# Shift and scale multiplied from unsplit weights in four column groups, and the modulation sums one product later

## The chip, the cores and the metric

One Trainium2 chip, one of its cores. The time is the device time of one execution in microseconds (us); the median of several runs counts. Traces are one profiled execution each, taken by the hardware profiler.

## The reference

Two transformer blocks over 256 tokens of 1024 features, in float32, with 256 context tokens beside them in the first block. Only its opening matters here:

```python
m_l = (silu(c) @ w_ada + b_ada)[:, None, :]       # of the tokens; w_ada is 1024 x 6144
m_c = silu(c_ctx) @ w_ada + b_ada                 # of the context
sh1, sc1, g1, sh2, sc2, g2 = jnp.split(m_l, 6, axis=-1)
csh1, csc1, *_ = jnp.split(m_c, 6, axis=-1)
hl = rmsnorm(lat, norm_g0) * (1.0 + sc1) + sh1
hc = rmsnorm(cx, norm_g0) * (1.0 + csc1) + csh1
... = jnp.split(h @ w_in, 5, axis=-1)             # q, f forward, f backward, v, g
```

Then come the HGRN2 mixer (a gated scan in both directions), the sum `lat + g1 * y`, a convolutional feed-forward part, and a second block of retention, windowed attention and an MLP. Only the token rows go on after the mixer.

## The kernel before

Everything runs on one core, and TensorE is kept supplied by a single stream of weights. The order of the work is written out by hand: instructions stand on each engine in the order in which the Python code emits them.

**The stream.** All weights are listed once, in the order of use, as chunks of one or two halves of up to 128 x 1024 numbers. `pump` (L115) walks that list: SP's queue issues the load of a half into one of eight `raw` buffers, as soon as the half eight places earlier is done with; then ScalarE (ACT) copies it to `hi` in float32r (L154), and VectorE (DVE) writes `lo = raw - hi` (L155), so that `hi + lo` is exact. A product is three float32r multiplications, hi times hi, hi times lo and lo times hi (`mm3`, L355 to L357, in these rows with the activations `hTh` and `hTl`). A half of kind "split" gives its raw buffer back when it is split, one of kind "raw" when its readers are done. `use` (L166) takes the next chunk and runs `pump`.

**The opening.** `xT` holds context and tokens with features on partitions, 512 columns for each of eight tiles k of 128 features. DVE and ACT square and add them (L452 to L456), four small multiplications (L466) sum over partitions, DVE and POOL make the reciprocal root `r` (POOL's power at L322), DVE puts `r` on four diagonals `dg` (L471), and a multiplication by ones (L480) spreads it over all partitions in PSUM; `x_r` multiplies a tile by it (L405). For each k, `ada_mm(k)` (L396) multiplies `silu` of the two conditioning vectors by the 1024 x 256 weights that give shift and scale of the 128 features of tile k. The vectors stand in `c4` as four columns, hi and lo of each, so that 16 multiplications of 4 output rows by 256 columns, hi (L399) and lo (L400) of the weights, make a result of four rows; ACT copies it to `rs` (L402). `feat(k)` (L407) multiplies `rs` by the small matrix `sel`, which adds the rows of one vector and turns the result so that features lie on partitions (L409, L410); DVE makes the factors `AB` (L412, L413); ACT and DVE write the normed tile in two parts, `hTh` and `hTl`.

**The steps.** The first product of the mixer, the gates of two heads (four output tiles `e` of 512 columns), is summed over k as the tiles get ready. Step k multiplies tile k by chunk `f0_k`; `plan` (L493) sets what else is emitted in it: "0s123a" is output 0, then `s` (feat and splits of tile k + 1), outputs 1 to 3, then `a` (`ada_mm(k + 2)`). In the stream the two halves of `ada` k + 2 stand between `f0_k` and `f0_k+1`.

**The rest of the modulation.** The other columns of `w_ada` are multiplied on DVE, a row tile at a time, into `vr`, between the mixer's products (`ada_step`, L559). When a part is complete, a function that finishes it waits in `pending` until `ada_flush` (L579). For g1 that is `ada_rows` (L588): two multiplications by ones that sum `vr` over partitions (L592, 512 columns each), each followed by an addition on DVE (L593).

**The gate product.** The last of the mixer's four head pairs has its small products among the columns of the gate product `g`, which has four parts p: `slots` (L862) puts the transposes T, the scores SC, the states S and the outputs O into it, one slot after every four k tiles. `SC_` (L631) multiplies 32-column stationary parts, with 128 rows, into the four 32-partition quarters of a bank (L640, L642); `S_` (L622) reads `kcT`, which ACT copies from the transposes (L620). After part p = 1 the code calls `ada_flush` (L878). PSUM banks with the tag `x` are four, taken in turn by these small products, by `ada_rows` and by `ada_mm`.

```python
        z = fm_product(C["g", p], x=lambda k: hT(k, 256, 512), tag="m", ticks=1)
        drain()
        if p == 1:
            ada_flush()
```

Of the kernel before, what the change touches and what calls it, by code (L numbers as in the profile page):

```python
# [13 lines left out]
OP = mybir.AluOpType  # L14
# [17 lines left out]
LAG2 = 3  # L32

# [17 lines left out]
def kernel(ctx: ExitStack, tc: tile.TileContext, a, out):  # L51
# [17 lines left out]
    # A chunk is one or two halves of up to 1024 columns. A half is loaded, then split exactly into two  # L69
    # float32r parts, hi + lo.  # L70
    halves, chunks = [], []

    def add(hs, kind="split"):
        """hs: per half (parts, k tiles, columns); a part is (view of the half's tile, source)."""
        first = len(halves)
        for parts, k, n in hs:
            halves.append((parts, k, n, kind))
            assert k * n <= 1024, (k, n)
        chunks.append((first, len(halves)))
        return len(chunks) - 1  # L80
# [4 lines left out]
    def kpc(src):  # L85
        return src.rearrange("(k p) c -> p k c", p=128)
# [13 lines left out]
    class SplitPool:  # L100
        """Buffers for the two parts of bufs halves, for the halves under limit."""
# [13 lines left out]
    def pump(limit, hold=False):  # L115
        """Issue the loads and the splits that have a free buffer, splits of halves under limit only."""
# [49 lines left out]
    def use(i, keep=None, ahead=None):  # L166
        """The k tiles of chunk i as a list of (hi, lo); chunks before it (or before keep) are done with."""
# [17 lines left out]
    def part_done(i):  # L185
        """The first half of chunk i is done with."""
        at_["rel"] = max(at_["rel"], chunks[i][0] + 1)
        pump(len(halves))

# [24 lines left out]
    def ada_chunk(k):  # L214
        C["ada", k] = add([([(lambda t, s=s: t[:, :, s * 128:(s + 1) * 128],
                              kpc(w_ada[j * 512:(j + 1) * 512, s * D + k * 128:s * D + (k + 1) * 128]))
                             for s in range(2)], 4, 256) for j in range(2)])
# [5 lines left out]
    for k in range(KT):  # L223
        C["f0", k] = add([([(lambda t, d=d: t[:, 0, d * 256:(d + 1) * 256],
                             w_in[k * 128:(k + 1) * 128, (1 + d) * D:(1 + d) * D + 256])
                            for d in range(2)], 1, 512)])
        if k + 2 < KT:
            ada_chunk(k + 2)
# [72 lines left out]
    sel = early.tile([4, 2], F32, name="sel")  # L301
# [22 lines left out]
    def rstd_of(ms, width=1, n=1):  # L324
        """(ms / n + eps) ^ -0.5; ms [128, width], or [128, 2] to be added."""
# [8 lines left out]
    def mean_sq(junk, x, ms):  # L334
        """ms = the part of the mean over D of x ^ 2 that x holds."""
        s_.activation(junk, x, AF.Square, scale=D ** -0.5, accum_out=ms)
# [43 lines left out]
    def fm_product(chunk, nk=KT, x=None, tag="x", ticks=0):  # L380
        """Two feature tiles of a product over lat tokens -> one bank [128, 2, T]."""
# [14 lines left out]
    def ada_mm(k, w):  # L396
        rw = bank("x")
        for kk in range(KT):
            t_.matmul(rw[:4, :256], c4[:, kk, :], w[kk][0], start=kk == 0, stop=False)  # L399
            t_.matmul(rw[:4, :256], c4[:, kk, :], w[kk][1], start=False, stop=kk == KT - 1)  # L400
        rs[k] = p0.tile([4, 256], F32, tag="rs", name="rs")
        return lambda: s_.activation(rs[k], rw[:4, :256], AF.Copy)  # L402
# [44 lines left out]
    # rstd of the tokens, then the same on every partition  # L447
    sq = [p0.tile([128, 512], F32, tag="sq", name="sq", bufs=8) for _ in range(KT)]
    c4 = early.tile([128, KT, 4], F32R, name="c4")
    for k in range(KT):  # L450
        if k < 2:
            v_.tensor_mul(sq[k], xT[:, k, :], xT[:, k, :])  # L452
        else:
            s_.activation(sq[k], xT[:, k, :], AF.Square)
            v_.tensor_add(sq[k % 2], sq[k % 2], sq[k])
    v_.tensor_add(sq[0], sq[0], sq[1])  # L456
    v_.tensor_mul(cs, cs, vecs[:, 0:16])
    for j in range(2):
        v_.tensor_copy(c4[:, :, 2 * j], cs[:, 8 * j:8 * j + 8])
        v_.tensor_tensor(c4[:, :, 2 * j + 1], cs[:, 8 * j:8 * j + 8], c4[:, :, 2 * j].bitcast(F32),  # L460
                         op=OP.subtract)
# [8 lines left out]
    for i in range(4):  # L470
        v_.tensor_scalar(dg[:, i, :], ident, r[:, i:i + 1], None, op0=OP.mult)  # L471
# [20 lines left out]
    # products of the gates, with the sums (a), the features (s) and the next weights' splits among them  # L492
# [66 lines left out]
    def ada_step(parts=(3, 4, 2)):  # L559
        """One chunk of the rest of the modulation: sums over k on each partition, then over partitions."""  # L560
# [146 lines left out]
    for p in range(4):  # L707
# [59 lines left out]
        def gates(d):  # L767
            kt_ = kk_[d]
            # ctx: k times the decay from its token to the end of the scan
# [15 lines left out]
            # lat: sums of log f within chunks of 64  # L785
# [38 lines left out]
            # tokens of a block in order: forward [A, B], backward [B, A], A scanned first;  # L824
            # the middle slot holds q of B from the block's start, k of A to the block's end
# [33 lines left out]
    # the last pair's products among those of the gate, as its factors get ready  # L859
# [13 lines left out]
    for p in range(4):  # L873
# [4 lines left out]
        if p == 1:  # L878
            ada_flush()
# [14 lines left out]
    def row_product(name, n, lhs, done):  # L894
        """Sums over k tiles of two; lhs(j, kk, tok) gives the stationary parts. The last chunks
        are taken token tile by token tile, so that the first tile's rows are finished early; done(tok, acc)
        is stepped as the halves of a tile's rows get ready, its last step gives what has to follow."""
# [64 lines left out]
    def to_hT(pool, n, tok, A, B=None, tag="hf"):  # L962
        """n [128, D] token rows -> hT columns of the token tile, times A (plus B) per feature.
        A bank is read by one engine only."""
# [29 lines left out]
    def scaled(dst, src, r):  # L994
        """dst = src * r, a half on each of two engines."""
# [29 lines left out]
    def split_rows(cs_, mid, first):  # L1025
        """The products of chunks of columns token tile by token tile, the second after mid(), which comes
        behind the first chunks of the first; gives what turns them, features on partitions."""
# [49 lines left out]
    def ffn_done(tok, acc):  # L1077
# [11 lines left out]
        # with v = mean(x^2) + eps, x v^-.5 g is the block's result, and its own norm u (mean(u^2) + eps v)^-.5  # L1089
# [18 lines left out]
    def conv(z, m, name):  # L1108
        """z [128, 2, T]: centred taps over the tokens of tiles m, m + 1."""
# [53 lines left out]
    # ---------------- second block: projections  # L1163
# [151 lines left out]
    # softmax and retention among the projections, a step after each four k tiles  # L1315
# [126 lines left out]
def _pack(inputs):  # L1442
    """The small vectors with features on partitions: column j of a vector holds features 128 j .. 128 j + 127."""
# [13 lines left out]
def _shape_constants():  # L1457
    ident = np.eye(128, dtype=np.float32)
    sel = np.array([[1, 0], [1, 0], [0, 1], [0, 1]], np.float32)
# [36 lines left out]
```

## Time and profile before

| | |
|---|---|
| time, median of 3 runs | 888.44 us (887.88 to 889.48) |
| profiled execution, span from first to last instruction | 886.7 us, 15396 instructions |
| profiled execution's own time | not listed apart from its span; the median lies 1.7 us above that |
| PE (matmul) busy | 863.0 us, 97% |
| PEld (weight load) busy | 781.0 us, 88% |
| DVE, ACT, POOL busy | 618.6, 512.9 and 17.3 us |
| bytes moved | 161.98 MB, 183 GB/s over the span |

Engines: PE is TensorE, PEld its weight loads, DVE is VectorE, ACT is ScalarE, POOL is GpSimd, SP the queue that issues most loads. Matmuls are pipelined, so that a row's duration includes the way through the array; the distance between starts is what one costs in a run of them. A multiplication of float32 operands is one instruction in the program and two records in the trace.

### The profile page before, as it was taken

The page shows a single profiled execution, that of the slowest core. Times are in us where ns is not written, and L with a number is a line of the kernel's source. Part 1 is how long each engine was busy: PE and PEld are TensorE (multiplying, and loading weights), DVE is VectorE, ACT ScalarE, POOL GpSimd, SP SyncE. Part 2 cuts the span into 40 slices and gives each one's busy share as a digit, 9 for nine tenths or more (in the row PEclk, how much of TensorE's full clock was granted, in tenths as well). Part 3 has the DMA queues.
Part 4 walks back from the last instruction along what each step waited for, and adds up shares of the span by engine and source line. Part 5 has one row for each costly group of instructions (what it writes and reads, how often), then busy time and mean ns, then how long its engine had stood idle before and what let it go on. Part 6 is the DMA issues. An engine that isn't in the chain of part 4 may idle for free.

```text
span 886.7 us, 15396 instructions
## 1 busy us (share of the span) xinstructions
PE 863.0 (97%) x6144; PEld 781.0 (88%) x6144; DVE 618.6 (70%) x955; ACT 512.9 (58%) x823; POOL 17.3 (2%) x27
## 2 busy tenths in 40 slices
PE   4999999999999999999999999999999999999997
PEld 2679897988978999999998799999999899999995
DVE  7876878776888778977767736766486587555532
ACT  6877575673857575655545745756463575444431
POOL 1000000000000000000000000000000000000000
PEclk9999999999999999999999999999999999999999
DMA  9984472733634458776764374445596087656401
GB/s 313 276 280 167 131 250 78 258 116 116 216 122 156 154 192 294 253 246 208 236 213 95 122 225 138 130 141 158 184 312 195 24 285 243 191 190 190 161 1 47
DMA packets 131967, 161.98 MB, mean 183 GB/s; under 512 B 14136, under 2 KB 114488, under 8 KB 131896
## 3 DMA queue, kind: packets, MB, share of 16 engines
q1 hardware_dynamic: 129728, 155.80, 55.0%
q10 hardware_dynamic: 2168, 5.20, 1.7%
q8 instruction: 48, 0.79, 0.3%
q14 instruction: 23, 0.19, 0.1%
HBM read 159.93 MB, written 1.05 MB: 182 GB/s over the span
## 4 chain that ended last, share of the span: by engine, by line
PE 91%; ACT 3%; DVE 3%; DMA 2%; issue 1%; POOL 0%; SPq 0%; POOLq 0%; DVEq 0%; ACTq 0%
PE m L355 17%; PE m L356 17%; PE m L357 17%; PE x L355 8%; PE x L357 8%; PE x L356 8%; PE x L684 2%; DMA xT<-in_xcT_dram 1%; PE m L345 1%; PE x L345 1%; PE m L346 1%; PE m L341 1%; PE x L626 1%; PE x L346 1%; DMA raw<-in_hg_w_in_dram 1%; PE x L341 1%
## 5 line engine op out<-in xcount | busy, mean ns | idle before, releaser
L155 DVE TENSOR_TENSOR lo<-raw,hi 128x1024 fp32r<-128x1024 f32 (+1 forms) x264 | 310.0, 1204 | 134.0 <-ACT hi L154 131.0
L154 ACT ACTIVATE hi<-raw 128x1024 fp32r<-128x1024 f32 (+1 forms) x264 | 265.7, 1038 | 121.1 <-PE x L356 51.0
L355 PE MATMUL m<-hTh,hi 128*128 128x256 f32 (+1 forms) x560 | 178.8, 319 | 0.6 <-ACT hTh L425 0.6
L356 PE MATMUL m<-hTl,hi 128*128 128x256 f32 (+1 forms) x560 | 171.7, 307 | 0.2 <-DVE hTl L432 0.2
L357 PE MATMUL m<-hTh,lo 128*128 128x256 f32 (+1 forms) x560 | 171.4, 306 | 0.0
L355 PE MATMUL x<-hTh,hi 128*128 128x256 f32 x592 | 166.2, 281 | 0.0
L356 PE MATMUL x<-hTl,hi 128*128 128x256 f32 x592 | 165.1, 279 | 0.0
L357 PE MATMUL x<-hTh,lo 128*128 128x256 f32 x592 | 165.1, 279 | 0.0
L355 PEld LDWEIGHTS m<-hTh,hi 128*128 128x128 f32 x560 | 105.8, 189 | 9.2 <-issue 2.9
L355 PEld LDWEIGHTS x<-hTh,hi 128*128 128x128 f32 x592 | 111.2, 188 | 1.0 <-ACT hi L154 0.2
L356 PEld LDWEIGHTS x<-hTl,hi 128*128 128x128 f32 x592 | 110.8, 187 | 1.0 <-issue 0.2
L357 PEld LDWEIGHTS x<-hTh,lo 128*128 128x128 f32 x592 | 111.2, 188 | 0.0
L356 PEld LDWEIGHTS m<-hTl,hi 128*128 128x128 f32 x560 | 105.8, 189 | 5.7 <-DVE hTl L432 0.8
L357 PEld LDWEIGHTS m<-hTh,lo 128*128 128x128 f32 x560 | 105.4, 188 | 5.8 <-DVE lo L155 0.4
L355 PE MATMUL m<-hi,ah 128*128 128x512 f32 x248 | 97.2, 392 | 0.0
L357 PE MATMUL m<-hi,al 128*128 128x512 f32 x248 | 96.8, 391 | 0.0
L356 PE MATMUL m<-lo,ah 128*128 128x512 f32 x248 | 96.5, 389 | 0.0
L357 PEld LDWEIGHTS m<-hi,al 128*128 128x128 f32 x248 | 46.5, 188 | 10.6 <-DVE al L1141 0.4
L356 PEld LDWEIGHTS m<-lo,ah 128*128 128x128 f32 x248 | 46.6, 188 | 8.9
L355 PEld LDWEIGHTS m<-hi,ah 128*128 128x128 f32 x248 | 46.6, 188 | 8.9 <-ACT ah L1137 0.2
L355 PE MATMUL m<-hi,hTh 128*128 128x256 f32 x128 | 36.2, 283 | 0.0
L575 DVE SCALAR_TENSOR_TENSOR vr<-raw,cs,vr 128x1024 f32<-128x1024 f32 x28 | 35.8, 1280 | 0.4
(302 smaller groups left out, 1267.4 us busy)
## 6 DMA issues: line engine op xcount, KB each, us to landing
raw<-in_ffn_w_up_dram SPq DMA_DIRECT2D x44, 512.0 KB, 5.7
raw<-in_w_in_dram SPq DMA_DIRECT2D x42, 512.0 KB, 3.6
raw<-in_hg_w_in_dram SPq DMA_DIRECT2D x36, 512.0 KB, 4.9
raw<-in_w_ada_dram SPq DMA_DIRECT2D x32, 512.0 KB, 4.9
raw<-in_w_up_dram SPq DMA_DIRECT2D x32, 512.0 KB, 4.7
raw<-in_w_down_dram SPq DMA_DIRECT2D x32, 512.0 KB, 3.6
raw<-in_ffn_w_down_dram SPq DMA_DIRECT2D x22, 512.0 KB, 4.5
raw<-in_w_ada_dram SPq DMA_DIRECT2D x32, 256.0 KB, 4.5
```

The lines of the kernel that those rows point to most:

```text
L154: s_.activation(h[:, :w], r[:, :w], AF.Copy)
L155: held.append(lambda r=r, h=h, l=l, w=w: v_.tensor_tensor(l[:, :w], r[:, :w], h[:, :w].bitcast(F32), op=OP.subtract))
L341: t_.matmul(o, hTl[:, k, c], w[k][0], start=False, stop=k == KT - 1)
L345: t_.matmul(o, hTh[:, k, c], w[k][0], start=k == 0, stop=False)
L346: t_.matmul(o, hTh[:, k, c], w[k][1], start=False, stop=False)
L355: t_.matmul(o, wh, xh, start=start, stop=False)
L356: t_.matmul(o, wh, xl, start=False, stop=False)
L357: t_.matmul(o, wl, xh, start=False, stop=stop)
L575: v_.scalar_tensor_tensor(acc, w[kk][0], cs[:, k:k + 1], acc, op0=OP.mult, op1=OP.add)
L626: t_.matmul(z[:, d * 128:(d + 1) * 128], kcT[hh][:, (2 * d + j) * 128:(2 * d + j + 1) * 128], vt[:, j, hh * 128:(hh + 1) * 128], start=j = ...
L684: t_.matmul(z[:, b * 128:(b + 1) * 128], l, r, start=i == 0, stop=i == len(terms) - 1)
```

## The change

- `w_ada`'s columns for the first shift and scale are laid out on the host (`ada1`), so that a half is one load with 4 KB per partition, and so are the `f0` chunks (`f0w`, 2 KB per partition); before, a half of either was two loads.
- The `ada` chunks are of kind "raw": they are not split, and the multiplication is of plain float32.
- `c4` (four float32r columns) gives way to `c2`, 32 float32 columns of which two are filled. `ada_mm` multiplies k tile kk into the partitions 32 (kk mod 4) to 32 (kk mod 4) + 31 of a bank, and `sel`, now 128 x 2, adds the four groups. `rs` has 128 rows.
- 36 multiplications of `ones` by `ones` (float32, 128 columns) stand ahead of the first sums, into a bank that nothing reads.
- `silu` of the vectors is computed after the fourth square, not after the last; the diagonals `dg` take one DVE instruction, not four.
- `ada_flush` is called after part p = 2 of the gate product, not after p = 1.

```diff
+WARM = 36
     def ada_chunk(k):
-        C["ada", k] = add([([(lambda t, s=s: t[:, :, s * 128:(s + 1) * 128],
-                              kpc(w_ada[j * 512:(j + 1) * 512, s * D + k * 128:s * D + (k + 1) * 128]))
-                             for s in range(2)], 4, 256) for j in range(2)])
+        C["ada", k] = add([([(whole, a["ada1"][k, :, j])], 4, 256) for j in range(2)], "raw")
...
-        C["f0", k] = add([([(lambda t, d=d: t[:, 0, d * 256:(d + 1) * 256],
-                             w_in[k * 128:(k + 1) * 128, (1 + d) * D:(1 + d) * D + 256])
-                            for d in range(2)], 1, 512)])
+        C["f0", k] = add([([(whole, a["f0w"][k])], 1, 512)])
...
-    sel = early.tile([4, 2], F32, name="sel")
+    sel = early.tile([128, 2], F32, name="sel")
...
         for kk in range(KT):
-            t_.matmul(rw[:4, :256], c4[:, kk, :], w[kk][0], start=kk == 0, stop=False)
-            t_.matmul(rw[:4, :256], c4[:, kk, :], w[kk][1], start=False, stop=kk == KT - 1)
-        rs[k] = p0.tile([4, 256], F32, tag="rs", name="rs")
-        return lambda: s_.activation(rs[k], rw[:4, :256], AF.Copy)
+            g = slice(kk % 4 * 32, kk % 4 * 32 + 32)
+            t_.matmul(rw[g, :256], c2[:, kk, :], w[kk][0], start=kk < 4, stop=kk >= 4)
+        rs[k] = p0.tile([128, 256], F32, tag="rs", name="rs")
+        return lambda: s_.activation(rs[k], rw[:, :256], AF.Copy)
...
-    c4 = early.tile([128, KT, 4], F32R, name="c4")
+    c2 = early.tile([128, KT, 32], F32, name="c2")
+    v_.memset(c2, 0.0)
+    wb = bank("x")
+    for _ in range(WARM):
+        t_.matmul(wb[:, 0:128], ones, ones, start=True, stop=True)
...
+        if k == 3:
+            for j in range(2):
+                v_.tensor_mul(c2[:, :, j], cs[:, 8 * j:8 * j + 8], vecs[:, 8 * j:8 * j + 8])
+            v_.tensor_mul(cs, cs, vecs[:, 0:16])
     v_.tensor_add(sq[0], sq[0], sq[1])
-    v_.tensor_mul(cs, cs, vecs[:, 0:16])
-    for j in range(2):
-        v_.tensor_copy(c4[:, :, 2 * j], cs[:, 8 * j:8 * j + 8])
-        v_.tensor_tensor(c4[:, :, 2 * j + 1], cs[:, 8 * j:8 * j + 8], c4[:, :, 2 * j].bitcast(F32),
-                         op=OP.subtract)
...
-    for i in range(4):
-        v_.tensor_scalar(dg[:, i, :], ident, r[:, i:i + 1], None, op0=OP.mult)
+    v_.tensor_tensor(dg, ident.rearrange("p (o c) -> p o c", o=1).to_broadcast([128, 4, 128]),
+                     r.rearrange("p (i o) -> p i o", o=1).to_broadcast([128, 4, 128]), op=OP.mult)
...
-        if p == 1:
+        if p == 2:
             ada_flush()
...
-    sel = np.array([[1, 0], [1, 0], [0, 1], [0, 1]], np.float32)
+    sel = np.tile(np.eye(32, 2, dtype=np.float32), (4, 1))
...
+    ada = np.asarray(inputs["w_ada"])[0, :, :2 * D].reshape(2, 4, 128, 2, KT, 128)
+    data["ada1"] = ada.transpose(4, 2, 0, 1, 3, 5).reshape(KT, 128, 2, 4, 256)
+    f0w = np.asarray(inputs["hg_w_in"])[0, :, D:3 * D].reshape(KT, 128, 2, D)[..., :256]
+    data["f0w"] = f0w.reshape(KT, 128, 1, 512)
```

What stands on PE between two outputs of a step: first the end of step 0 before (of the 16 multiplications of `ada_mm` eight are shown; the lines of the changed kernel are three fewer there than before), with `c_150` the columns `c4`,

```order
L356 MATMUL m<-hTl,hi 128x512
L357 MATMUL m<-hTh,lo 128x512
L399 MATMUL x<-hi,c_150 4x256
L400 MATMUL x<-lo,c_150 4x256
L399 MATMUL x<-hi,c_150 4x256
L400 MATMUL x<-lo,c_150 4x256
L399 MATMUL x<-hi,c_150 4x256
L400 MATMUL x<-lo,c_150 4x256
L399 MATMUL x<-hi,c_150 4x256
L400 MATMUL x<-lo,c_150 4x256
```

and the same place in the changed kernel, with `c_142` the 32 columns of `c2`, as far as the feat of the next step:

```order
L353 MATMUL m<-hTl,hi 128x512
L354 MATMUL m<-hTh,lo 128x512
L397 MATMUL x<-raw,c_142 32x256 x8
L352 MATMUL m<-hTh,hi 128x512
L353 MATMUL m<-hTl,hi 128x512
L354 MATMUL m<-hTh,lo 128x512
L406 MATMUL x<-sel,rs 128x2
L407 MATMUL x<-sel,rs 128x2
```

Eight multiplications read the raw weights where 16 read their two parts; nothing else on PE moved within a step.

ACT in two steps of the opening, before (`h` and `hTh` are the features, `rs` the result of `ada_mm`, `hi` the weights' upper parts):

```order
L154 ACTIVATE hi<-raw 128x1024
L402 ACTIVATE rs<-x 4x256
L154 ACTIVATE hi<-raw 128x512
L154 ACTIVATE hi<-raw 128x1024
L423 ACTIVATE h<-xT,AB 128x256 x2
L428 ACTIVATE hTh<-h 128x512
```

and in the changed kernel:

```order
L399 ACTIVATE rs<-x 128x256
L155 ACTIVATE hi<-raw 128x512
L420 ACTIVATE h<-xT,AB 128x256 x2
L425 ACTIVATE hTh<-h 128x512
```

The two copies of 1024 columns per step are gone, and with them, on DVE, the two subtractions; the split of `f0` still stands ahead of the features.

PE at the end of part p = 1 of the gate product, before (the scores SC of the last head pair, then `ada_rows`, then part p = 2):

```order
L642 MATMUL x<-qe,ke 32x32
L645 MATMUL x<-Q,K 128x128
L651 MATMUL x<-Q,K 64x64 x2
L592 MATMUL x<-vr,ones 128x512 x2
L355 MATMUL m<-hTh,hi 128x256
L356 MATMUL m<-hTl,hi 128x256
```

and in the changed kernel, at the end of part p = 2:

```order
L643 MATMUL x<-qe,ke 32x32
L646 MATMUL x<-Q,K 128x128
L652 MATMUL x<-Q,K 64x64 x2
L593 MATMUL x<-vr,ones 128x512 x2
L352 MATMUL m<-hTh,hi 128x256
L353 MATMUL m<-hTl,hi 128x256
```

The two sums, and on DVE their two additions, stand 48 multiplications and four small products later; at the end of p = 1 the scores are followed by part p = 2 at once.

## Rows read from the trace of the kernel before

**Rows 1.** The page's chain that ended last, by engine.

```profile
PE 91%; ACT 3%; DVE 3%; DMA 2%; issue 1%; POOL 0%; SPq 0%; POOLq 0%; DVEq 0%; ACTq 0%
```

**Rows 2.** Waits of PE, whole span: total us, times, longest us.

```profile
PE x L592 <- ACT kcT L620: 1.8, 1, 1.8
...
PE x L409 <- ACT rs L402: 0.6, 1, 0.6
```

**Rows 3.** Timeline, step 4: start us, duration us, engine, line, out<-in.

```profile
45.05 0.39 PE L355 MATMUL m<-hTh,hi 128*128 128x512 f32 x1
...
45.84 0.38 PE L409 MATMUL x<-sel,rs 4*128 4x2 f32 x2
...
46.37 0.50 PE L355 MATMUL m<-hTh,hi 128*128 128x512 f32 x1
...
48.57 0.28 PE L399 MATMUL x<-hi,c 128*4 128x256 f32 x1
...
48.78 0.69 DVE L432 TENSOR_TENSOR hTl<-h,hTh 128x512 fp32r<-128x512 f32 x1
...
50.39 0.39 PE L355 MATMUL m<-hTh,hi 128*128 128x512 f32 x1
```

**Rows 4.** Timeline of all engines, from the first sums to the last step.

```profile
13.48 0.37 PE L399 MATMUL x<-hi,c 128*4 128x256 f32 x1
...
13.91 2.05 POOL L322 TENSOR_TENSOR r<-r,mhalf 128x4 f32<-128x4 f32 x1 [13.46 <-DVE r L330]
...
16.66 0.41 PE L400 MATMUL x<-lo,c 128*4 128x256 f32 x1
...
16.92 2.02 PE L480 MATMUL x<-dg,ones 128*128 128x512 f32 x2
16.93 2.95 DVE L155 TENSOR_TENSOR lo<-raw,hi 128x1024 fp32r<-128x1024 f32 x3
...
19.80 0.68 DVE L405 TENSOR_TENSOR xT<-xT,x 128x512 f32<-128x512 f32 x1
...
21.97 0.50 PE L355 MATMUL m<-hTh,hi 128*128 128x512 f32 x1 [0.56 <-ACT hTh L425]
...
61.88 0.39 PE L357 MATMUL m<-hTh,lo 128*128 128x512 f32 x1
```

**Rows 5.** Timeline of PE, scores in four 32-column groups of the array.

```profile
96.47 0.40 PE L357 MATMUL m<-hTh,lo 128*128 128x512 f32 x1
96.80 0.24 PE L640 MATMUL x<-qe,ke 128*32 128x64 f32 x1
...
96.82 0.25 PE L642 MATMUL x<-qe,ke 128*32 128x32 f32 x3
...
97.16 0.49 PE L645 MATMUL x<-Q,K 128*128 128x128 f32 x2
```

**Rows 6.** Timeline of PE, one float32 product of 256 columns: both records, then the first alone.

```profile
531.41 0.59 PE L1220 MATMUL x<-ks,qs 64*128 64x256 f32 x2
...
531.41 0.38 PE L1220 MATMUL x<-ks,qs 64*128 64x256 f32 x1
```

**Rows 7.** Windows: stretch, length, busy us by engine, granted clock, DMA share, GB/s.

```profile
13.40:16.80 3.40, 3.40 (x18) 1.85 (x17) 2.45 (x8) 2.48 (x3) 2.05 (x1) 1.00 1.12 344
...
250.90:254.20 3.30, 3.30 (x11) 2.27 (x11) 3.30 (x5) 1.10 (x2) 0.00 (x0) 0.50 0.30 102
```

**Rows 8.** Timeline around the modulation sums: PE, ACT, DVE.

```profile
247.72 1.12 PE L592 MATMUL x<-vr,ones 128*128 128x512 f32 x2
250.62 1.88 PE L592 MATMUL x<-vr,ones 128*128 128x512 f32 x2 [1.78 <-ACT kcT L620]
...
264.56 0.39 PE L355 MATMUL m<-hTh,hi 128*128 128x256 f32 x1
...
249.98 1.08 ACT L620 ACTIVATE kcT<-x 128x512 f32<-128x512 f32 x2
...
250.88 1.22 DVE L155 TENSOR_TENSOR lo<-raw,hi 128x1024 fp32r<-128x1024 f32 x1
```

## The prediction

> **What bounds the kernel now.** I read the chain that ended last first, then PE's waits, then the stretches that the change touches. PE carries 91% of the chain that ends last [rows 1], in a span of 886.7 us. PE's waits are few: the longest in the body of the kernel is 1.8 us, of the modulation sums on ACT's `kcT`; the next one in the opening is 0.6 us, of a feat on `rs` [rows 2]. So microseconds taken off PE come off the time, as long as ACT, DVE and the loads keep up, and I look at three places: the start, the eight steps of the opening, and the sums for g1.
>
> In a step of the opening the reader is to see that PE is full: from 45.05 to 50.39, 5.34 us, three products, the feat at 45.84, nine products from 46.37 to 48.57 (0.24 us each), sixteen small ones of `ada_mm` from 48.57 to 50.39 (1.82 us, 0.114 each), and the next step follows at once [rows 3]. The steps run from 21.97 to 61.88 and 0.23 for the last product: 40.1 us [rows 4]. Without waits they would take six times 5.34, once 3.52 (step 6, no `ada_mm`) and once 2.9 (step 7, no feat): 38.4 us. So 1.7 us are waits, mostly in the first three steps, where splits on ACT and DVE hold things up.
>
> **The steps.** `ada_mm` becomes eight float32 products of 256 columns, 16 records. Two such records took 0.59 and one 0.38, so they follow each other by 0.21 us [rows 6]. What is not plain is whether four column groups run at once. The scores show it: 16 records, of which a group with 64 columns has four, began at 96.80, the first of each group by 96.82, and the next full-width product began at 97.16 [rows 5]. One after the other, at 0.21 per 256 columns, eight records of 64 and eight of 32 columns would take 0.64 us; four at once, 0.21, which leaves 0.15 for start and end. The scores also began 0.33 after a product that costs 0.24, 0.09 late. So `ada_mm` should take 0.09 + 4 x 0.21 + 0.15 = 1.1 us instead of 1.82. For the six in the steps: 6 x 0.72 = 4.3 us saved.
>
> The Trainium skill ("TensorEngine Tiling (Array Packing)", Key Properties) says that a change of the tiling mode drains the array; the 0.09 and the 0.15 are what this trace shows of it. Its page "TensorE: Matmul & The Clock Gate" (Measured speedup vs the span model) gives a speedup of 3.07 for four row tiles, not 4; an estimate from that page is 1.3 us instead of 1.1, and 1.4 us less saved over the six.
>
> Of the 1.7 us of waits I take 1.5 as gone. ACT loses two copies per step and DVE two subtractions; only the features' own chain stays, and it fits: feat to next step's second product is now 0.53 + 9 x 0.24 + 1.1 + 0.24 = 4.0 us, against 3.6 us from the feat at 45.84 to the end of `hTl` at 49.47 [rows 3]. What is late next would be that chain, with 0.4 us of slack. **Together 5.8 us;** bounds 3.0 (a group costs half again as much and the waits stay) and 6.0.
>
> **The loads.** A step needs 1.31 MB. With the queue full, 344 GB/s were moved even in the present short pieces [rows 7], 3.8 us per step against a new pace of 4.6, and the pieces get longer. A raw half is now held until PE has multiplied it, not until DVE has split it, and SP issues in order, so the third `f0` load waits for `ada_mm(1)`. Eight buffers are two and two thirds steps, some 12 us, which covers the load. I take nothing; the queue behind SP is a rival below.
>
> **The start.** Sixteen products from 13.48 to 16.66 are 0.21 us apart [rows 4], where the same ones take 0.114 later [rows 3]: half pace, 1.2 GHz against 2.4, although the window prints 1.00 [rows 7]; where the page prints 0.50, the pace is the same. The added 36 products are 72 records of 128 columns, 0.105 us each at full clock and 0.21 at half. They can begin near 1.1. If the clock rises after as long as the 0.50 stretch lasted, 3.3 us [rows 7], 16 records go at half and 56 at full: done at 10.3, before the squares at about 12. If it takes twice as long, done at 11.8. All at half would be 16.2.
>
> Then the sums run at full pace, which with three small products moved into DVE's chain of squares brings POOL's power (13.91) forward by some 0.3 us; and `x_r` no longer waits for three subtractions (16.93 and 2.95) but follows the spread `r`, which ends at 18.94: 0.8 earlier than 19.80 [rows 4]. That makes 1.1. If the spread too ran at full pace it would be 1.0 more. But `ada_mm(0)` is shorter now, so PE idles for POOL's 2.05 us between it and the spread; an idle time of 1.78 was followed by a granted clock of 0.50 [rows 7, 8]. So I expect half pace again, and charge 0.4 for the first products of step 0 (1.4 if all of them are slow). **0.7 us;** bounds -0.3 and 2.1.
>
> **The modulation sums.** Before, the first of the two sums ran at 247.72; the second needed a bank that ACT had not yet emptied, and began at 250.62 after 1.78 us of idle. Then 3.3 us went by at a granted clock of 0.50, half of it lost, and part p = 3 began at 264.56 [rows 7, 8]. Of the 16.84 us between, 1.78 + 1.65 are loss and 13.4 are work. All this work remains, in another order. What is late next: part p = 2 starts at 247.8, twelve products take 1.4 us, and then the states S need the same `kcT`, whose first half ACT ends at about 250.5, and soon after the `lo` that DVE ends at 252.1 [rows 8]. ACT and DVE do not wait for PE there, so this does not move: 1.3 + 0.5 = 1.8 us of new idle. At the new place, after p = 2, the banks that the sums take were emptied long before, and DVE's two additions fall where it has idle time. **Saved: 16.84 - 13.4 - 1.8 = 1.6 us,** if the clock stays. PE idled 0.6 us once without a loss of clock [rows 2] and 1.78 once with it; 1.3 is between. I take it as staying, since it is shorter than the only one that cost the clock; if not, nothing is saved. Bounds 0 and 3.4.
>
> **Sum.** 5.8 + 0.7 + 1.6 = 8.1 us, so a span of about 878.6. The median before, 888.44, lies 1.7 above the profiled span, and I take the same here: **880.3 us**. By the bounds: 11.5 saved, 876.9, and 2.7 saved, 885.7.
>
> **Rivals.**
>
> 1. *The two records of a product hold back the next group.* The trace speaks against it: four groups' first records began within 0.02 us, before any second one could [rows 5]. If it were so here, with 256 columns, a group would start when the one before is half done: 9 x 0.21 + 0.24 = 2.1 us per `ada_mm`. The steps would lose 6 x 0.3 = 1.8, gain the 1.5 of waits, the start would lose 0.5 of its 0.7: 1.4 saved in all, 887.0, no change that can be told. The Trainium skill's page "TensorE: Matmul & The Clock Gate" (The mechanism) has matmuls start and end strictly in program order; by that rule this rival would hold, and these rows differ from it. Chance 0.06.
> 2. *Wide streams do not run side by side at all.* The rows in four groups are of 32 and 64 columns; four streams of 256 float32 columns at once are not in this trace. In a row they cost 16 x 0.21 + 0.24 = 3.6 us, 1.78 more than now; six make 10.7, `ada_mm(1)` 1.5 more ahead of step 0; against 1.5 + 0.7 + 1.6 saved that is 8.4 lost: 896.8. It decides from 1.82 us per `ada_mm` on. Chance 0.06.
> 3. *SP's order starves the steps.* If each step waits for its load and keeps 5.34 us, only the start and the sums save, 2.3: 886.1. Against it stand 344 GB/s and the eight buffers. Chance 0.05.
> 4. *The added products outlast the squares* and end at 16.2: 3.9 of the 8.1 are lost, 884.2. Chance 0.03.
>
> **How the numbers follow.** My forecast has 0.80. The range, 876.5 to 885.5, takes in its bounds, less a few tenths at the worst end where all three would have to fail together, and rival 4; it leaves out the first three. A measurement of this kernel can tell some 0.2%, 1.8 us, from no change: its three runs spread over 1.6. Faster by more than that is below 886.7: the forecast, rivals 3 and 4, 0.88. Within it: rival 1, 0.06. Slower: rival 2, 0.06.
>
> **What would show it.** Each `ada_mm` as 16 records that begin in groups of four and take 1.0 to 1.2 us up to the next full-width product, steps of 4.6 us, the first at about 20.9, the last ending near 55.5. No subtraction of 1024 columns on DVE in the opening. A short wait of PE on `kcT`, by the states S, and no wait of the modulation sums. A granted clock of 1.00 after it. It would be wrong if `ada_mm` takes 2 us or more, if PE waits for DMA or for `hi` in the steps, or if steps and start save their share and the stretch from 56 to 240 gives it back.

## The result and the profile after

The changed kernel takes 880.29 us (median of 4 runs, 877.26 to 882.56); the kernel before takes 888.16 us beside it (median of 4, 887.13 to 889.48). The ratio is 0.9906, interval 0.9886 to 0.9927. The prediction was 880.3 us. The total was met, but not term by term: the start was put too low, the steps and the sums too high, and by luck these misses nearly cancel.

The profiled run is the fastest of the four: 877.26 us with a span of 875.5 us. Its chain still lies on TensorE, with a smaller share than [rows 1]. From the page:

```profile
PE 89%; DVE 5%; ACT 3%; DMA 1%; issue 1%; POOL 0%; SPq 0%; POOLq 0%; DVEq 0%; ACTq 0%
```

PE's waits, to be read against [rows 2] (total us, times, longest us):

```profile
PE m L352 <- ACT hTh L422: 1.5, 1, 1.5
PE x L627 <- ACT kcT L621: 1.4, 1, 1.4
...
PE x L481 <- DVE dg L471: 1.1, 1, 1.1
...
PE x L699 <- DVE on L693: 0.5, 1, 0.5
...
PE x L685 <- ACT xs L665: 0.4, 1, 0.4
```

The sums' own wait of 1.8 us is gone from the list. The states S (L627) wait for `kcT` instead, as the prediction had it. Two waits later in the same stage are new: O (L685) and its transposes (L699). In the start PE now waits for `dg` and for the first features.

The start, to be read against [rows 4]. Timelines of PE, DVE, POOL and ACT (start us, duration us, engine, line):

```profile
12.02 1.03 PE L467 MATMUL x<-ones,sq 128*128 128x2 f32 x8
12.98 1.07 PE L397 MATMUL x<-raw,c 128*32 128x256 f32 x16
15.13 1.12 PE L481 MATMUL x<-dg,ones 128*128 128x512 f32 x2 [1.08 <-DVE dg L471]
...
19.12 0.50 PE L352 MATMUL m<-hTh,hi 128*128 128x512 f32 x1 [1.52 <-ACT hTh L422]
...
25.62 0.50 PE L352 MATMUL m<-hTh,hi 128*128 128x512 f32 x1
```

```profile
13.34 1.02 POOL L319 TENSOR_TENSOR r<-r,mhalf 128x4 f32<-128x4 f32 x1 [12.90 <-DVE r L327]
...
15.68 0.63 ACT L155 ACTIVATE hi<-raw 128x512 fp32r<-128x512 f32 x1 [1.17 <-DMA raw<-in_f0w_dram]
...
16.34 0.69 DVE L156 TENSOR_TENSOR lo<-raw,hi 128x512 fp32r<-128x512 f32 x1 [1.10 <-ACT hi L155]
...
16.95 0.68 DVE L402 TENSOR_TENSOR xT<-xT,x 128x512 f32<-128x512 f32 x1
```

The sums, the small products and the spread run at full pace: 1.03, 1.07 and 1.12 us, where the spread took 2.02 [rows 4]. The first gate product stands at 19.12 us instead of 21.97, and step 1 begins at 25.62. What held `x_r` (L402) was no longer three subtractions but one, L156, behind a load.

Step 4 and the last gate product, to be read against [rows 3] and [rows 4] (timeline of PE and DVE):

```profile
38.87 0.50 PE L352 MATMUL m<-hTh,hi 128*128 128x512 f32 x1
...
39.44 0.40 PE L354 MATMUL m<-hTh,lo 128*128 128x512 f32 x1
39.67 0.28 PE L406 MATMUL x<-sel,rs 128*128 128x2 f32 x2
39.81 0.36 PE L407 MATMUL x<-sel,rs 128*128 128x2 f32 x2
40.03 0.47 PE L352 MATMUL m<-hTh,hi 128*128 128x512 f32 x1
...
42.28 1.07 PE L397 MATMUL x<-raw,c 128*32 128x256 f32 x16
42.45 0.69 DVE L429 TENSOR_TENSOR hTl<-h,hTh 128x512 fp32r<-128x512 f32 x1 [1.23 <-ACT hTh L425]
...
43.28 0.50 PE L352 MATMUL m<-hTh,hi 128*128 128x512 f32 x1
...
54.24 0.39 PE L354 MATMUL m<-hTh,lo 128*128 128x512 f32 x1
```

`ada_mm` takes 42.28 to 43.28, 1.00 us. A step takes 38.87 to 43.28, 4.41 us, where 4.6 was predicted and 5.34 measured before. The feat fell too, from 0.53 us [rows 3] to 0.36 (39.67 to 40.03).

Matching each product with its counterpart before tells where the time came from. The first gate product is 2.85 us earlier, the last one (54.24 against 61.88) 7.64 earlier. From there to 236 us PE waits for nothing in either kernel, and the lead grows by another 1.3 us, mostly by the pace of the 256-column products, which also differs between runs of one kernel (below).

### The profile page after: what moved, and what is told of

The parts are those of the page before. It is cut to its first block, busy times and chain, and to the rows that moved or that the text cites. A ratio compares the mean times of both kernels' runs of the same rounds, so it can differ in the third digit from the quotient of the medians.

```text
span 875.5 us, 15429 instructions
## 1 busy us (share of the span) xinstructions
PE 859.9 (98%) x6216; PEld 780.3 (89%) x6216; DVE 599.5 (68%) x935; ACT 497.7 (57%) x807; POOL 16.3 (2%) x27
## 4 chain that ended last, share of the span: by engine, by line
PE 89%; DVE 5%; ACT 3%; DMA 1%; issue 1%; POOL 0%; SPq 0%; POOLq 0%; DVEq 0%; ACTq 0%
PE m L352 17%; PE m L354 17%; PE m L353 17%; PE x L352 8%; PE x L354 8%; PE x L353 8%; PE x L685 1%; DVE lo L156 1%; PE m L342 1%; PE x L342 1%; PE m L343 1%; PE m L338 1%; DMA raw<-in_f0w_dram 1%; PE x L343 1%; PE x L338 1%
## 5 line engine op out<-in xcount | busy, mean ns | idle before, releaser
L156 DVE TENSOR_TENSOR lo<-raw,hi 128x1024 fp32r<-128x1024 f32 (+1 forms) x248 | 291.0, 1203 | 130.7 <-ACT hi L155 130.6
L155 ACT ACTIVATE hi<-raw 128x1024 fp32r<-128x1024 f32 (+1 forms) x248 | 249.6, 1039 | 117.6 <-PE x L353 50.7
```

What stands on the lines that cost most here:

```text
L155: s_.activation(h[:, :w], r[:, :w], AF.Copy)
L156: held.append(lambda r=r, h=h, l=l, w=w: v_.tensor_tensor(l[:, :w], r[:, :w], h[:, :w].bitcast(F32), op=OP.subtract))
```

## The experiments

A label stands for one kernel; "the changed kernel" is the one after the change. Every ratio is to the kernel before on the same chip.

**The changed kernel once more**, as the measure of the next three.

> The changed kernel once more, beside the three below, as their measure: 880.3 us (877.3 to 882.6 before). Both theories: the whole gain lies in the first stage (start of the q products at 54.5 us instead of 62.1), and the times of single runs differ by the number of stretches of about 3.4 us at half clock (1.7 us each): a run with a mean granted clock of 0.991 is 5 us longer than one of 0.997.

879.83 us (6 runs, 878.59 to 882.33), ratio 0.9916 (0.9900 to 0.9932). In the profile the clock fell to half at 14.25 us for 6.8 us, where the first profile has it at 20.61 for 3.4 us; the first gate product came at 19.44. The spread took 2.08 us there, at half, as the prediction had it. So where in the opening the clock falls changes from run to run, but in both it falls. The time agrees with the share of the clock only roughly: 0.991 took 882.56 and 0.997 took 877.26 of the first four, but 0.995 appears here with 878.59 and 880.84.

**The sums back behind part p = 1 of the gate product** (e1; the expectation calls the part a pair), **and the move alone** (e2).

```diff
 e1, on the changed kernel          e2, on the kernel before
-        if p == 2:                 -        if p == 1:
+        if p == 1:                 +        if p == 2:
             ada_flush()                         ada_flush()
```

> Only the move of the sums undone (behind the product of pair 1 again). Theory: the move was worth 0.2 us net, since the waits of the third pair's steps on DVE and ACT gave back what the idle before them had cost; so 880.5 us against the changed kernel's 880.3, and the stretch at half clock at about 245 us is back or not by chance. Rival (the prediction's own term): 1.6 us slower, 881.9 us.

> The move of the sums alone, on the kernel before. Theory: no difference, 888 us within 0.5 of the kernel before on the same chip, because the wait of 1.8 us and the half-clock stretch go and the waits for kcT, xs and DVE come. Rival (the prediction's term): 1.6 us faster.

e1: 880.31 us (6 runs), ratio 0.9918 (0.9900 to 0.9937), not to be told from the changed kernel. e2: 888.84 us (12 runs), ratio 1.0005 (0.9991 to 1.0018): a gain of more than 0.8 us is excluded, so the term of 1.6 us falls. Matched products say what little there is. Between the last product ahead of the sums in either place and the first of the output projection, e1 lost 0.22 us on the changed kernel and e2 gained 0.59 on the one before. PE of e1 around its sums:

```profile
239.34 1.12 PE L593 MATMUL x<-vr,ones 128*128 128x512 f32 x2
...
242.40 1.18 PE L593 MATMUL x<-vr,ones 128*128 128x512 f32 x2 [1.94 <-ACT kcT L621]
```

Its clock also fell to half at 243.34 for 3.4 us, and by the product at 245.3 it had fallen 4.8 us behind the changed kernel's second profile. Some 2 us of that are the sums' own work, which the changed kernel still has to do; at the output projection the two were level again but for 0.2 us. What the changed kernel pays in between stands in its first profile, PE and then DVE:

```profile
241.93 1.16 PE L627 MATMUL x<-vt,kcT 128*128 128x128 f32 x8 [1.38 <-ACT kcT L621]
...
252.39 1.98 PE L593 MATMUL x<-vr,ones 128*128 128x512 f32 x4
256.12 0.49 PE L685 MATMUL x<-St,Q 128*128 128x128 f32 x2 [0.38 <-ACT xs L665]
...
264.89 0.59 PE L699 MATMUL x<-ident,on 128*128 128x128 f32 x2 [0.51 <-DVE on L693]
```

```profile
258.34 1.28 DVE L594 TENSOR_TENSOR vr<-vr,x 128x512 f32<-128x512 f32 x2
259.54 0.68 DVE L885 TENSOR_TENSOR oTs<-oTs,sg 128x512 f32<-128x512 f32 x1
260.14 0.68 DVE L871 TENSOR_TENSOR yl<-oTs,yh 128x512 fp32r<-128x512 f32 x1
260.75 1.22 DVE L156 TENSOR_TENSOR lo<-raw,hi 128x1024 fp32r<-128x1024 f32 x1
261.88 0.16 DVE L327 TENSOR_SCALAR r<-ss 128x2 f32<-128x2 f32 x1
```

The sums' additions (L594) stand on DVE ahead of three more pieces of work and of the norm (L327) that the transposes wait for. DVE was not idle at the new place: it works without a gap from the additions to that norm. In e10 below the wait for `kcT` was taken away as well.

**No products ahead of the sums** (e3).

```diff
-WARM = 36
+WARM = 0
```

> The 36 products of ones ahead of the norm's sums left out. Theory: sums, first small products and spread run at half clock again; only the spread (1.12 us at full clock, 2.02 us at half) is on the path, the small products lie under waits for DVE and ACT, so 0.9 us slower: 881.2 us, first gate product at 20.0 us instead of 19.1. Rival: the products only shift the stretch at half clock from the spread into the first gate products, so without them step 0 runs at full clock sooner and the time is the same, 880.3 us. A second rival: all products up to the first gate ones and 3 us of these run at half, 2.5 us slower.

879.24 us (5 runs, 879.08 to 880.06), ratio 0.9909 (0.9895 to 0.9923): the first rival. The first gate product is 0.95 us later than in the first profile, as the theory had it, but the clock rises at 17.38 us and stays (a window ahead of that prints 1.00, as in [rows 7], though the products there run at half pace), so no half-clock stretch follows in step 0. PE of this run, at the start of steps 0 and 1:

```profile
20.07 0.51 PE L352 MATMUL m<-hTh,hi 128*128 128x512 f32 x1 [0.88 <-ACT hTh L422]
...
24.98 0.50 PE L352 MATMUL m<-hTh,hi 128*128 128x512 f32 x1
...
26.09 0.50 PE L354 MATMUL m<-hTh,lo 128*128 128x512 f32 x1 [0.38 <-DVE lo L156]
```

Step 0 takes 4.91 us here and 6.50 in the first profile (19.12 to 25.62). In step 1 PE then waits 0.38 us for the `lo` of the gate weights, which stands on DVE behind the features' work, and the lead is gone (26.80 against 26.79 us). In the change as it stands, the 36 products bring nothing.

**The waits of the start filled** (e6).

```diff
+    for _ in range(3):
+        t_.matmul(rb[:, 0:128], ones, ones, start=True, stop=True)
     t_.matmul(rb, ones, dg.rearrange("p a b -> p (a b)"), start=True, stop=True)
...
     x_r(1, R)
+    for _ in range(4):
+        t_.matmul(zf[0][:, 0:128], ones, ones, start=True, stop=True)
```

> Three products of ones in TensorE's wait for the diagonal (1.08 us) and four in its wait for the first features (1.52 us), 0.31 us each, overwritten by the product that follows in the bank. Theory: the stretch at half clock at 20.6 to 24.0 us comes from these two waits; with them filled it is gone, 1.7 us faster: 878.6 us, half-clock stretch absent from the first 60 us of the profile. Rival: the clock falls there whatever TensorE did in the 2.6 us before; 880.3 us and a stretch at half clock at about 20 us stays.

878.10 us (5 runs, 876.99 to 878.61), ratio 0.9890 (0.9876 to 0.9905): 1.7 us less than the changed kernel beside it, as the theory had it. In the profiles the q products, the first behind the steps, begin at 53.26 us instead of 54.47 and 54.18. The windows from 12 to 18 and 18 to 24 us, first of the changed kernel's second profile, then of this one (stretch, length, busy us of PE, PEld, DVE, ACT and POOL, granted clock, DMA share, GB/s):

```profile
12.00:18.00 6.00, 4.92 (x34) 2.99 (x37) 2.58 (x8) 1.01 (x2) 1.02 (x1) 0.69 1.01 387
18.00:24.00 6.00, 6.00 (x40) 3.73 (x36) 2.71 (x8) 3.78 (x8) 0.00 (x0) 0.74 0.96 364
```

```profile
12.00:18.00 6.00, 5.79 (x57) 3.92 (x58) 2.94 (x10) 1.35 (x3) 1.02 (x1) 1.00 1.03 402
18.00:24.00 6.00, 5.50 (x38) 3.66 (x38) 3.21 (x8) 3.88 (x9) 0.00 (x0) 1.00 0.98 390
```

The seven products do no useful work; they lie in waits that are there anyway, and the clock stays at 1.00. This profile has a half-clock stretch at 243.26 us too, behind the same wait for `kcT` as in the changed kernel, whose clock stayed there: 1.4 us were lost by 248 us against the changed kernel's second profile, and at the output projection all of it was caught up.

**The same without the 36 products** (e11): e6 with `WARM = 0`.

> The kernel with the two waits filled, but without the 36 products of ones ahead of the norm's sums. Theory: these products pay only together with the filled waits: filled, they keep full clock from about 4 us on (878.1 us); without them sums, small products and spread run at half clock until about 17 us and the first gate product comes 0.9 us later, 879.0 us. Rival: the filling products alone bring the clock up in time, so the first gate product stays within 0.3 us of 18.8 us and the time at 878.1 us.

880.16 us (4 runs, 879.77 to 880.59), ratio 0.9911 (0.9894 to 0.9927). Slower than the filled kernel, as the theory had it, but by 2.1 us and not by 0.9. The clock rose only at 19.42 us, so the three filling products ran at half pace and outlasted the wait they were meant to fill:

```profile
16.29 1.65 PE L482 MATMUL x<-ones 128*128 128x128 f32 x6
17.73 1.87 PE L483 MATMUL x<-dg,ones 128*128 128x512 f32 x2
...
21.83 0.50 PE L352 MATMUL m<-hTh,hi 128*128 128x512 f32 x1
```

The two runs were on different chips, but each stands against the kernel before on its own. The 36 products and the filled waits are worth something only together.

**All small products in one group** (e4).

```diff
-            g = slice(kk % 4 * 32, kk % 4 * 32 + 32)
-            t_.matmul(rw[g, :256], c2[:, kk, :], w[kk][0], start=kk < 4, stop=kk >= 4)
+            t_.matmul(rw[:32, :256], c2[:, kk, :], w[kk][0], start=kk == 0, stop=kk == KT - 1)
...
```

> All eight small products of a step in the first group of 32 columns, one behind the other; everything else as changed (the features' products then read 32 rows instead of 128). Theory: the four groups work side by side, and that is what makes a step's small products 1.00 us; in one group they take 3.6 us (the prediction's second rival), so six steps on TensorE's path are 2.6 us longer each and the time is about 880 + 16 = 896 us. Rival: an unsplit product of 32 columns is short by itself and the groups are not needed: 1.0 us, 880 us.

895.98 us (2 runs), ratio 1.0086 (1.0065 to 1.0106). One step's small products in its PE timeline:

```profile
32.94 3.64 PE L396 MATMUL x<-raw,c 128*32 128x256 f32 x16
36.51 0.51 PE L352 MATMUL m<-hTh,hi 128*128 128x512 f32 x1
```

3.57 us instead of 1.00. Unsplit products pay here only because four groups share the array; in one group the change would have been a loss.

**Consecutive products in the same group** (e5).

```diff
-            g = slice(kk % 4 * 32, kk % 4 * 32 + 32)
-            t_.matmul(rw[g, :256], c2[:, kk, :], w[kk][0], start=kk < 4, stop=kk >= 4)
+            g = slice(kk // 2 * 32, kk // 2 * 32 + 32)
+            t_.matmul(rw[g, :256], c2[:, kk, :], w[kk][0], start=kk % 2 == 0, stop=kk % 2 == 1)
```

> Two consecutive products in each group (0, 0, 1, 1, 2, 2, 3, 3 instead of 0, 1, 2, 3, 0, 1, 2, 3). Theory, the prediction's first rival by itself: products start in program order, so the second of a pair waits for the first and holds back the other groups; 2.1 us per step instead of 1.0, about 880 + 6.6 = 887 us. Rival: groups take their products independently of the order in which these were written; 1.0 us, 880 us.

880.03 us (2 runs), ratio 0.9906 (0.9886 to 0.9926). In its PE timeline:

```profile
32.89 1.09 PE L397 MATMUL x<-raw,c 128*32 128x256 f32 x16
33.91 0.50 PE L352 MATMUL m<-hTh,hi 128*128 128x512 f32 x1
```

1.02 us in this order against 1.00 in the other. In both, the sixteen records begin in four rounds of four, about 0.21 us apart. The trace does not name the group of a record; that a round holds one of each group is read from e4, where the records of one group begin 0.21 us apart. The prediction's first rival is out; so is, for products in different column groups, the rule of the Trainium skill named beside it in the prediction ("TensorE: Matmul & The Clock Gate", The mechanism).

**Features from 4 rows instead of 128** (e7).

```diff
-    t_.matmul(ab[:, 0:2], rs[k][:, 0:128], sel, start=True, stop=True)
+    t_.matmul(ab[:, 0:2], rs[k][:4, 0:128], sel[:4, :], start=True, stop=True)
...
```

> The two products that turn the sums into features read 4 rows of the sums, as before the change, instead of 128 (only the first group's sums then count: three quarters of each sum are left out). Theory: the 0.16 us by which a step's pair fell (0.53 to 0.37 us) is the number of rows; with 4 rows it is 0.53 us again, 7 times, so 1.0 us slower, 881 us. Rival: it fell because of what stands ahead of it (unsplit products in place of split ones); it stays at 0.37 us, 880 us.

881.41 us (2 runs), ratio 0.9922 (0.9902 to 0.9941). The two products of a step, in its PE timeline:

```profile
40.45 0.40 PE L354 MATMUL m<-hTh,lo 128*128 128x512 f32 x1
40.77 0.38 PE L406 MATMUL x<-sel,rs 4*128 4x2 f32 x2
41.02 0.36 PE L407 MATMUL x<-sel,rs 4*128 4x2 f32 x2
41.30 0.51 PE L352 MATMUL m<-hTh,hi 128*128 128x512 f32 x1
41.65 0.39 PE L353 MATMUL m<-hTl,hi 128*128 128x512 f32 x1
```

They take 0.53 us again (40.77 to 41.30), as the theory had it. They also begin 0.32 us after the product ahead of them, where the changed kernel has 0.23 (39.44 to 39.67). The step takes 4.71 to 4.72 us, 0.30 longer: nearly twice what the theory had counted. The time itself is not to be told from the changed kernel's.

**The shift and scale weights loaded in the old pieces** (e8).

```diff
-        C["ada", k] = add([([(whole, a["ada1"][k, :, j])], 4, 256) for j in range(2)], "raw")
+        C["ada", k] = add([([(lambda t, s=s: t[:, :, s * 128:(s + 1) * 128],
+                              kpc(w_ada[j * 512:(j + 1) * 512, s * D + k * 128:s * D + (k + 1) * 128]))
+                             for s in range(2)], 4, 256) for j in range(2)], "raw")
```

> The unsplit shift and scale weights loaded as before the change, in two pieces of 128 columns per half from the full matrix, instead of one piece of a repacked array. Theory: loads were in time in both kernels, TensorE waits for none of them in the first 60 us, so 880 us (within 0.5). Rival, the prediction's third: twice the pieces keep the queue behind SP longer, a step of the first stage starts late by up to 1 us each, 886 us.

881.51 us (4 runs, 881.15 to 881.76), ratio 0.9921 (0.9905 to 0.9938): 1.2 to 1.7 us above the changed kernel's medians, though the intervals overlap. The rival's 886 us is out, and the theory that nothing changes fails in the trace. The steps do not starve. What comes late is the first load of gate weights, queued behind the pieces. ACT and DVE in the start:

```profile
17.02 0.63 ACT L155 ACTIVATE hi<-raw 128x512 fp32r<-128x512 f32 x1 [2.43 <-DMA raw<-in_f0w_dram]
...
17.69 0.69 DVE L156 TENSOR_TENSOR lo<-raw,hi 128x512 fp32r<-128x512 f32 x1 [2.37 <-ACT hi L155]
...
18.30 0.68 DVE L404 TENSOR_TENSOR xT<-xT,x 128x512 f32<-128x512 f32 x1
```

Everything from `hi` on is 1.35 us later than in the changed kernel, and so is the first gate product (20.47). PE did not wait for the load by name, so the list of its waits could not show it: it waited for `hTh`, and `hTh` for `x_r`, which stood behind that `lo` on DVE. Behind PE's wait of 2.78 us for `hTh` the clock was at half from 20.97 us for 6.8 us, twice as long as in the first profile; how much of the time is the load and how much the clock is not separated.

**The first gate weights loaded earlier** (e9), on the filled kernel, **and the states S one slot later** (e10), on e9, which its expectation calls the kernel before.

```diff
 e9:
     ada_chunk(0)
+    C["f0", 0] = add([([(whole, a["f0w"][0])], 1, 512)])
     ada_chunk(1)
     for k in range(KT):
-        C["f0", k] = add([([(whole, a["f0w"][k])], 1, 512)])
+        if k:
+            C["f0", k] = add([([(whole, a["f0w"][k])], 1, 512)])
...
-    w1 = use(C["ada", 1], keep=C["ada", 0], ahead=0)
     ev()
     w = use(C["f0", 0], keep=C["ada", 0], ahead=0)
+    w1 = use(C["ada", 1], keep=C["ada", 0], ahead=0)
 e10:
-    slots = [..., [[S0], [SC10, S1], [SC01], [SC11]], ...]
+    slots = [..., [[], [S0, SC10], [S1, SC01], [SC11]], ...]
```

> The kernel with the filled waits, and the first gate weights loaded ahead of the second shift and scale weights instead of behind them (two filling products instead of four ahead of the first gate product). Theory: in the changed kernel the first features hang on DVE, where the subtraction of the first gate weights (16.34 to 17.03 us, behind a load that lands at 15.7) stands ahead of the first norm product; with the load 3 us earlier that subtraction ends before the spread does, so the first gate product is some 0.7 us earlier than the 18.8 us of the filled kernel: 877.4 us. Rival: the second shift and scale weights now land late and hold the second batch of small products by as much; first gate product at 18.8 us or later, 878.1 us or more.

> The kernel before with, in addition, the state products S of the last pair one slot (twelve products, 1.4 us) later. Theory: the wait of 1.4 us for kcT ahead of them goes, but the stage up to 288 us is set by the chain on DVE and ACT (a stretch of 3.4 us at half clock at 243 us had vanished by 288 us), so at most 0.5 us comes off the time: 877.0 to 877.4 us. Rival: TensorE sets the stage and the wait comes off whole, 1.4 us: 876.0 us.

e9: 878.04 us (4 runs, 876.83 to 878.67), ratio 0.9880 (0.9863 to 0.9897). The first gate product comes at 18.44 us, 0.37 earlier than in the filled kernel and not 0.7. `x_r` now follows the spread, as the theory had it, but the norm's sums began 0.2 us later here (12.06 against 11.85), behind the last of the 36 products. The time cannot be told from the filled kernel's. e10: 879.59 us (4 runs), ratio 0.9902 (0.9888 to 0.9917): no gain, rather a loss. The wait for `kcT` is gone, and another has come:

```profile
242.46 0.58 PE L356 MATMUL m<-hTh,lo 128*128 128x256 f32 x1 [2.68 <-DVE lo L156]
```

The twelve products drawn ahead need the next weights' `lo`, and DVE, busy without a gap from 235.8 to 246.6 us in the changed kernel's second profile, does not come to them before 241.9. In e9 the same product begins at 242.58, so nothing was gained by taking the wait for `kcT` away: the part p = 2 is paced by DVE at this point, not by PE's order. What e10 lost came behind it: its clock was at half from 242.27 us for 3.4 us, and at the output projection it is 0.9 us behind e9's profile.

## Why the total was right and the terms were not

**The steps: mechanism right, sum 5.8 predicted, 4.8 measured** (from the first gate product to the last: 39.9 us before, 35.1 after). The four groups run at once; e4 and e5 show it by taking it away and by changing the order. `ada_mm` took 1.00 us; it enters 0.1 late and leaves its next product 0.11 us longer (0.34 to the second product instead of 0.23). Together that is 1.2 us, where the prediction had 1.1 with entry, start and end: 0.6 net instead of 0.72, 3.7 over six. The feat was put at no change; it gave 0.3 in each of seven steps, 2.1 us (e7). Of the waits, put at 1.5 gone, 1.2 went (steps 0 to 4 held 1.7 us of them before and 0.5 after), and 0.6 came at the first products of step 7, where the features' own chain ends last; the prediction had named that chain with 0.4 us of slack. Then 1.6 us went to the half clock in step 0 (6.50 us against 4.91 in e3's profile), which the prediction had charged to the start. Where the clock stays through step 0, 0.65 us of this is lost in step 1 instead, which takes 5.07 us and not 4.42 (e3; 5.05 in the second profile, whose half clock ends early in step 0): there PE waits for `lo`, so that the chain of features on ACT and DVE, and not PE, sets the pace.

**The start: 0.7 predicted, 2.85 measured at the first gate product (2.53 in the second profile), ahead of the half clock in step 0.** The sums ran at full pace, as forecast; so did the spread in the first profile, which was not. The half clock came as expected, only later, and its cost was put at 0.4 where this run paid 1.6. The power took 2.05 us on POOL before and 1.02 after. That is not the change's doing: e2, whose start is that of the kernel before, shows 1.02 too, and its first gate product comes 0.4 us earlier than the 21.97 of [rows 4]. POOL and PE of e2:

```profile
14.37 1.02 POOL L322 TENSOR_TENSOR r<-r,mhalf 128x4 f32<-128x4 f32 x1 [13.93 <-DVE r L330]
...
21.59 0.50 PE L355 MATMUL m<-hTh,hi 128*128 128x512 f32 x1 [0.88 <-ACT hTh L425]
```

So some 0.4 us of the 2.85 belong to the one profiled run before; how the rest splits between the clock, the load and DVE's shorter queue was not tested piece by piece. `x_r` did not follow the spread, as forecast, but a `lo` behind a load, 0.7 us later; e8 and e9 moved that load and moved the first gate product with it. The prediction took nothing for the loads; in the start the larger pieces are worth 1.35 us at the first gate product (e8).

**The modulation sums: 1.6 predicted, 0 to 0.6 measured** (e1, e2). The term that was mis-sized rests on the sentence that DVE's two additions fall where it has idle time, and on the count of late work: it took in `kcT` (1.3, measured 1.4) and `lo`, but not `xs` and the norm (0.4 and 0.5 us of waits). Against the kernel before, 1.7 us of lead is lost from the start of part p = 3 to the output projection. The clock stayed in both profiles of the changed kernel, as forecast, but behind the same wait it fell in e6's, so that this was luck in part. A half-clock stretch in this stage cost nothing in the end there, so its going was no gain.

**Rivals.** Rival 1 is out by e5, rival 2 by e4, which costs what it said (3.57 against 3.6 us, 896.0 against 896.8). Rival 3 did not occur in the steps; e8 shows its weaker form in the start. Rival 4 did not occur: the added products were over by 12.4 us in every profile that has them, though in three of them (e5, e8, e9) they held the sums up by 0.2 to 0.4 us.

So the total was met because the start brought some 2 us more than put down and the sums 1 to 1.6 less, with the steps 1 short; that these cancel is luck. Against the medians, 7.9 us were saved. Ahead of the q products the two profiles of the changed kernel lead that of the kernel before by 7.6 and 7.9 us. This measure is no firmer than one profiled run: e2, with the same opening as the kernel before, reaches the q products 1.1 us later than it (63.25 against 62.11), with a half-clock stretch of 3.4 us at 23.74, so that the kernel before can lose time to the clock in step 0 too.

## What to carry to other kernels

Small float32 products that leave most of the array's columns idle are worth spreading over column groups; both orders tried took the same time. Check the products beside them as well, since operands of few rows cost 0.3 us a step here. Work moved out of a wait gains only if the engine that releases the wait is not the pace of the stage: look at that engine's timeline for gaps before booking the wait as saved. Products that keep the clock up paid here only once the waits between them and the real work were filled as well.

## What was not expected of the hardware

- The 256-column products run at one of two paces in a stage, also in one kernel: from about 600 to 640 us they follow each other by 0.113 us in the first profile of the changed kernel and by 0.118 in its second (222 steps from one product to the next, from 609.77 to 634.93 and from 609.58 to 635.73 us), at a granted clock of 1.00 in both. The profiled pair differ by 11.2 us, 3.3 more than the medians, and this pace, in three stretches (62 to 247, 288 to 350 and 590 to 720 us of the kernel before), makes most of that. Why a stage takes one or the other stays open.
- An operand of 4 or 32 rows between products of 128 rows (e7, e4) costs time: it begins 0.32 us after the product ahead instead of 0.23, and its two pairs of records are 0.25 us apart instead of 0.14.
- Half-clock stretches lasted 3.4 us or 6.8 us in these traces. The start at full clock that was bought with 36 products was lost again behind short waits (half from 14.25 us, after 1.0 us of idling ahead of the sums and within the wait for `dg`; or from 20.61, after waits of 1.1 and 1.5 us), while the filled kernel, with 0.9 us idle ahead of the sums and 0.2 and 0.3 us after, kept it.
